# A two-layer trunk of three token mixers: state-space and output splits in slots of their own, the norm gain spread by products, a longer pause of the table work

## The chip, the core and the metric

The kernel runs on one core of a Trainium2 chip. The metric is the device time of one execution in microseconds (us), the median of several runs.

## What is computed

A residual stream x of 512 tokens by 1024 channels passes two layers. Cut to what matters here, a layer is:

```
h = rmsnorm(x, norm_g)                      # norm_g: 1024 gains, one row a layer
proj = h @ w_in                             # split into rq rk rv rz, sq sk sv sz, cu cz, ga gb gc
y_a = retention(rq, rk, rv) * silu(rz)      # 4 heads, chunks of 128
y_b = stick_breaking(sq, sk, sv) * silu(sz) # 8 heads of 64, strictly causal
y_c = s5_ssm(cu) * silu(cz)                 # scan over a complex state, gelu, then
                                            # y * sigmoid(y @ w_glu + b_glu)
merged = sigmoid(ga) * (y_a @ proj_a) + sigmoid(gb) * (y_b @ proj_b) + sigmoid(gc) * (y_c @ proj_c)
x = x + merged @ w_out
```

All is float32. A float32 product of large operands is made of three products of a 32-bit format that TensorE takes in one pass: each operand is split into a high part (a ScalarE copy, names ending in h) and a low part (operand minus high part, on VectorE, names ending in l), and hh, hl and lh are summed.

## The kernel before

**Slots.** A layer is a list of 108 main pieces, written out in `ORDER_TEXT`; a piece is 12 or 24 products of 512 columns (`mm`) that fill one PSUM bank. Here a slot is one piece with all that is emitted around it. The loop at the end of `layer` (from L1342) writes a slot in this order: first the helpers that are due (generators in `due`), then the piece, then the helpers' second halves (those that yielded 0, in `late`), then `W.fill()`, which splits coming weights (`wh` on ScalarE, `wl` on VectorE; weights are loaded as `raw` on SP's queue), then background work. A helper that yields n goes on n slots later. Nothing reorders after that: each engine runs its instructions in the order in which they were written, and waits on semaphores.

**Background.** In layer 0 it is `tables()` (powers of the state matrix, small VectorE products with buffers `dbl`, tables `cr`, `ci`, `fr`, `fi`) and then `coef.gen` (L672 on: coefficients of the scan, GpSimd products `ct`, `bbr`, `bbi`, `ab`, from four loads of 256 KB that ScalarE's queue issues); in layer 1 it is `coef.gen` alone. The loop pulls steps while two counters of emitted work, of GpSimd and of VectorE, stay below shares of the slot's TensorE work; a step that has nothing to do yet only raises the counter. In the slots of `quiet` (L1341) nothing is pulled: the slot of the first attention pair and the one before, and six slots at the fourth pair.

**Attention pairs.** `sb_pair(pr)` (L1017), pr 0 to 3, starts every four slots from the last `sv` on. It copies `qd` and `ks` on ScalarE and `ql`, `ks` on VectorE, and a GpSimd copy completes each `qd`. Then, slot by slot and for two heads, TensorE makes scores (`z`), ScalarE two sigmoids (`kp`, `w`), VectorE a scan over `kp` and the product into `w`, and TensorE turns `w` by transposes (`wt`), so TensorE waits for VectorE's `w` there. At its end the pair's output `sbo` is multiplied by the gate and split at once into `ybh`, `ybl`; they are read by the `pb` pieces, the first of them 13 slots after the first pair's split and five after that of the third.

**State space.** `ssm(q)` (L872), q 0 to 3, makes the branch's output `g[q]`. When q is 3, its end splits all four `g` into `gh`, `gl` in one slot (L955 on), waits two slots (`K["s7"]`) and multiplies each `g` by its gate `zc` on GpSimd. The `glu` pieces, after the four slots of `rv1`, read the splits; `glu_evac` multiplies `g` again. The split stands in the slot of the last `rv0`, where `W.fill` also makes the four weight units of `rv1`.

**Start.** `first_x` (L430) normalises the four token blocks of x. The gain must lie on all 128 partitions (`gB`, two tiles of 512 columns); `load_gain` (L424) reads the one row of 2 KB 128 times, by a broadcasting transfer for each tile, behind the first block of x in SP's queue and ahead of the first weights. A block is squared on ScalarE, its mean and root on GpSimd (`rs`), scaled on VectorE (`xn`), transposed on TensorE (`T`) and copied as `hh` and `hl`.

Of the kernel before, what the change touches and what calls it, by code (L numbers as in the profile page):

```python
# [10 lines left out]
F32 = mybir.dt.float32  # L11
# [3 lines left out]
ALU = mybir.AluOpType  # L15
PSUM = bass.MemoryType.PSUM

P = 128
# [17 lines left out]
K = dict(  # L36

    nw=12, w=4, raw=4, b=48,

    sb0=0, sb_gap=4, ssm0=6, ssm_gap=3, ret0=9, ret_gap=3, x0=-3, x1=2, ret_pre=4, lead=15,  # L40

    g=0.9, v=0.7,

    n1=1, n2=1, q1=1, q2=1, k1=1, k2=2, s1=1, s2=1, s3=1, s4=2, s5=1, s6=1, s7=2, b1=1, b2=1, b3=1,
# [142 lines left out]
def trunk(ctx: ExitStack, tc, x_in, w_in, par_in, bc_in, ng_in, cst_in, rope_in, out):  # L187
    nc = tc.nc
    load = {"V": 0.0, "G": 0.0, "T": 0.0}

    def counted(f, engine, each):


        def g(*a, **k):
            o = k["out"] if "out" in k else a[0]
            load[engine] += 0.07 * (engine != "T") + each * math.prod(o.shape[1:])
            return f(*a, **k)  # L197

        return g
# [4 lines left out]
    GT, GS = counted(nc.gpsimd.tensor_tensor, "G", 2.2e-3), counted(nc.gpsimd.tensor_scalar, "G", 1.2e-3)  # L204
# [11 lines left out]
    def bt(name, dt=F32, shape=(P, 512)):  # L216
        return bp.tile(list(shape), dt, tag="b", name=name)
# [7 lines left out]
    def psm(name):  # L225
        return ps_sm.tile([P, 512], F32, tag="sm", name=name)
# [14 lines left out]
    def C(n):  # L241
        o, s = CST[n]
        return cst[:, o : o + s]

    make_identity(nc, ident)
    make_identity(nc, identb)
    nc.gpsimd.memset(negm, -1e30)
    nc.gpsimd.affine_select(
        out=negm, in_=negm, pattern=[[1, P]], base=0, channel_multiplier=-1, compare_op=ALU.is_ge, fill=0.0
# [31 lines left out]
    def split(src, name, shape=(P, 512)):  # L281
        h = bt(name + "h", F32R, shape)
        l = bt(name + "l", F32R, shape)
        ACT(h, src, AF.Copy)  # L284
        TT(out=l, in0=src, in1=h.bitcast(F32), op=ALU.subtract)
        return h, l
# [137 lines left out]
    def load_gain(l, q=nc.scalar):  # L424
        gB = [bt("gB0"), bt("gB1")]
        for c in range(2):
            q.dma_start(out=gB[c], in_=ng_in[l, 512 * c : 512 * c + 512].partition_broadcast(P))
        return gB

    def first_x():  # L430
        xs = [[bt("x0"), bt("x1")] for t in range(NT)]
        gB = []

        def load(t):
            for c in range(2):
                nc.sync.dma_start(out=xs[t][c], in_=x_in[t * P : t * P + P, 512 * c : 512 * c + 512])

        load(0)
        gB.extend(load_gain(0, nc.sync))
        W.load(2)  # L440
        load(1)
        W.load(4)

        def block(t):
            ss = st("ss", 2)
            xn = [sum_square(xs[t][c], ss, c) for c in range(2)]
            yield from normalise(t, xs[t], xn, ss, gB)

        b = [block(t) for t in range(NT)]
        for i in range(3):  # L450
            next(b[0])
        W.make()
        next(b[0], None)
        next(b[1])
        W.make()
        next(b[1])
        load(2)
        W.make()
        load(3)
        W.make()  # L460

        def second():
            next(b[1])
            next(b[1], None)

        between.append(second)
        next(b[2])
        spawn(b[2], 0)
        spawn(b[3], 0)
# [340 lines left out]
    def layer(l, last, base):  # L810
# [59 lines left out]
        g = [None] * 4  # L870

        def ssm(q):  # L872
            win, ca, mt, T = coef.q[q]
            p0 = G * l + 8 * q

            pu = transposed(U[q])
            yield 0
            ut = bt("ut")
            for k in range(2):
                src = pu[64 * k : 64 * k + 64].rearrange("p (i c j) -> p i c j", i=4, j=2)  # L880
                for j in range(2):
                    dst = ut[64 * j : 64 * j + 64].rearrange("p (i k c) -> p i k c", i=4, k=2)
                    ACT(dst[:, :, k, :], src[:, :, :, j], AF.Copy)
            yield K["s1"]
            ps = psm("S")
            for n in range(8):
                sl = slice(n * 64, n * 64 + 64)
                MM(ps[:, sl], win[n // 4][:, n % 4 * P : n % 4 * P + P], ut[:, sl], start=True, stop=True)
            yield 0

            H, tm, tx = bt("H"), bt("tm"), bt("tx")
            lo, hi = slice(0, 64), slice(64, P)
            TT(out=tm, in0=ps, in1=T[0], op=ALU.mult)
            TT(out=tx[lo], in0=ps[hi], in1=T[1][hi], op=ALU.mult)
            TT(out=tx[hi], in0=ps[lo], in1=T[1][lo], op=ALU.mult)
            yield K["s2"]
            TT(out=tm, in0=tm, in1=tx, op=ALU.add)
            for n in range(8):
                sl = slice(n * 64, n * 64 + 64)
                nc.vector.tensor_tensor_scan(  # L900
                    tm[:, sl], r8[:, p0 + n : p0 + n + 1].to_broadcast([P, 64]), tm[:, sl], 0.0, ALU.mult, ALU.add
                )
            nc.gpsimd.memset(v3(H, 64)[:, :, 0:1], 0.0)
            yield K["s3"]

            def sh0(ap):
                return v3(ap, 64)[:, :, 0:63]

            def sh1(ap):
                return v3(ap, 64)[:, :, 1:64]  # L910


            TT(out=sh1(H), in0=sh0(tm), in1=sh0(T[0]), op=ALU.mult)
            TT(out=sh0(tx)[lo], in0=sh0(tm)[hi], in1=sh0(T[1])[hi], op=ALU.mult)
            TT(out=sh0(tx)[hi], in0=sh0(tm)[lo], in1=sh0(T[1])[lo], op=ALU.mult)
            TT(out=sh1(H), in0=sh1(H), in1=sh0(tx), op=ALU.subtract)
            yield K["s4"]

            py = psm("py")
            for i in range(4):  # L920

                for part in range(2):
                    for n in (i, i + 4):
                        sl = slice(n * 64, n * 64 + 64)
                        o = py[64 * (n // 4) : 64 * (n // 4) + 64, n % 4 * P : n % 4 * P + P]
                        k = 2 * (n % 2) + n // 4
                        if part == 0:
                            MM(o, ut[:, sl], mt[n % 4 // 2][:, k * P : k * P + P], start=True, stop=False)
                        else:
                            MM(o, H[:, sl], ca[:, n, 1:9, :].rearrange("p a b -> p (a b)"), start=False, stop=True)  # L930
            coef.used = q + 1
            yield 0
            ysb = bt("ysb")
            ACT(
                ysb.rearrange("p (j g m) -> p g j m", j=8, g=4), py.rearrange("p (g j m) -> p g j m", g=4, j=8), AF.Copy
            )
            yield K["s5"]
            pt = transposed(ysb)
            yield 0
            y = bt("y")  # L940
            for k in range(2):
                src = pt[64 * k : 64 * k + 64].rearrange("p (i h c) -> p i h c", i=4, h=2)
                for h in range(2):
                    dst = y[64 * h : 64 * h + 64].rearrange("p (c i k) -> p i c k", i=4, k=2)
                    ACT(dst[:, :, :, k], src[:, :, h, :], AF.Copy)

            u, sg = bt("gu"), bt("gs")
            ACT(u, y, AF.Square, scale=math.sqrt(0.044715))
            yield K["s6"]
            STT(out=u, in0=u, scalar=1.0, in1=y, op0=ALU.add, op1=ALU.mult)  # L950
            yield 0
            ACT(sg, u, AF.Sigmoid, scale=2.0 * math.sqrt(2.0 / math.pi))
            TT(out=y, in0=y, in1=sg, op=ALU.mult)
            g[q] = y
            if q == 3:  # L955
                yield 1
                for i in range(4):
                    gs[i] = split(g[i], "g")
                yield K["s7"]
                for i in range(4):  # L960
                    while zc[i] is None:
                        yield 1
                    GT(out=g[i], in0=g[i], in1=zc[i], op=ALU.mult)


        gs, yc, yb, mg, ya = [None] * 4, [None] * 4, [None] * 4, [None] * 8, [None] * 8
        zc, zb = [None] * 4, [None] * 4
# [49 lines left out]
        def sb_pair(pr):  # L1017
# [85 lines left out]
            for kb in range(4):  # L1103

                for h in range(2):
                    c = slice(128 * pr + 64 * h, 128 * pr + 64 * h + 64)
# [6 lines left out]
            while zb[pr] is None:  # L1113
                yield 1
            TT(out=sbo[pr], in0=sbo[pr], in1=zb[pr], op=ALU.mult)
            yb[pr] = split(sbo[pr], "yb")


# [127 lines left out]
        gB = []  # L1246
# [91 lines left out]

        first = at["sv"] + 3 + K["sb0"]
        turn = first + 3 * K["sb_gap"]  # L1340
        quiet = {*range(first - 1, first + 1), *range(turn, turn + 6)}  # L1341
        for name, m in mains:  # L1342
            i = now[0]
            quarters()
# [21 lines left out]
    while due:  # L1366
        i = min(due)
# [28 lines left out]
```

## Time and profile before

| | |
|---|---|
| median of three runs | 1303.77 us (1303.42 to 1303.91) |
| the profiled execution | 1303.42 us, its span 1301.7 us |
| TensorE (PE) busy | 1267.4 us, 97% of the span |
| VectorE (DVE) busy | 853.3 us, 66% |
| ScalarE (ACT) busy | 537.5 us, 41% |
| GpSimd (POOL) busy | 391.3 us, 30% |
| moved by DMA | 120.05 MB, mean 92 GB/s |

The page comes from one execution. PE is TensorE's products, PEld its weight loads. An engine's idle time matters only where it makes TensorE wait. Views with times are given from the span's start. The two layers run the same list of pieces, so layer 1 (from 661 us on) can be laid beside layer 0 (from 11 us on); a slot's length below is the time from its first product with weights to that of the next slot.

### The profile page before, as it was taken

What the parts mean: (1) busy time and instruction counts of PE and PEld (TensorE: products, weight loads), DVE (VectorE), ACT (ScalarE), POOL (GpSimd) and SP (SyncE); (2) the same over time, 40 slices, a digit from 0 to 9 for tenths busy, and PEclk for the clock granted to TensorE, in tenths of its full rate; (3) what the DMA queues carried; (4) which work ended last, traced back from release to release, by engine and by line L of the source; (5) the groups of instructions that cost most, each with busy time, mean ns of one, the idle gap of its engine ahead of it and who ended that gap; (6) DMA issues with size and microseconds to landing.
All of it is one profiled execution on the core that took longest, in us unless ns stands there. A gap on an engine that the chain in (4) does not pass through costs nothing. (4 is left out here: it accounts for less than half of the span.)

```text
span 1301.7 us, 16635 instructions
## 1 busy us (share of the span) xinstructions
PE 1267.4 (97%) x6360; PEld 1048.0 (81%) x6360; DVE 853.3 (66%) x1189; ACT 537.5 (41%) x919; POOL 391.3 (30%) x452
## 2 busy tenths in 40 slices
PE   7997999999999999999999998999999999999998
PEld 5886778888887888888888876888888878888887
DVE  5988795866785539556365578678657844575542
ACT  5453455445343533332244544534534534423311
POOL 3334351638442012000043136444565311210000
PEclk9998999999999999999999999999999999999999
DMA  6331222223322322234433222122232232122342
GB/s 225 94 134 49 65 68 75 69 82 97 114 65 65 113 78 69 81 97 142 162 118 129 81 66 65 49 82 81 89 106 65 74 121 82 65 81 81 97 135 75
DMA packets 37375, 120.05 MB, mean 92 GB/s; under 512 B 4144, under 2 KB 4528, under 8 KB 37296
## 3 DMA queue, kind: packets, MB, share of 16 engines
q1 hardware_dynamic: 29664, 105.40, 25.6%
q10 hardware_dynamic: 7632, 13.59, 3.1%
q8 instruction: 50, 0.82, 0.3%
q14 instruction: 29, 0.24, 0.1%
HBM read 114.78 MB, written 4.19 MB: 91 GB/s over the span
## 5 line engine op out<-in xcount | busy, mean ns | idle before, releaser
L197 DVE TENSOR_TENSOR wl<-raw,wh 128x1024 fp32r<-128x1024 f32 x196 | 253.6, 1302 | 115.8 <-ACT wh L318 112.8
L197 PE MATMUL mm<-hh,wh 128*128 128x512 f32 x640 | 256.4, 401 | 0.0
L197 PE MATMUL mm<-hh,wl 128*128 128x512 f32 x640 | 251.1, 392 | 0.0
L197 PE MATMUL mm<-hl,wh 128*128 128x512 f32 x640 | 251.0, 392 | 0.0
L318 ACT ACTIVATE wh<-raw 128x1024 fp32r<-128x1024 f32 x196 | 205.8, 1057 | 71.4 <-PE mm L197 38.9
L197 PE MATMUL mm<-wh,hh 128*128 128x512 f32 x512 | 206.6, 404 | 0.6 <-ACT hh L421 0.6
L197 PE MATMUL mm<-wl,hh 128*128 128x512 f32 x512 | 201.9, 394 | 4.3 <-DVE wl L197 4.3
L197 PE MATMUL mm<-wh,hl 128*128 128x512 f32 x512 | 201.4, 393 | 0.0
L197 PEld LDWEIGHTS mm<-hh,wh 128*128 128x128 f32 x640 | 121.1, 189 | 25.6 <-issue 1.8
L197 PEld LDWEIGHTS mm<-hh,wl 128*128 128x128 f32 x640 | 120.8, 189 | 26.0
L197 PEld LDWEIGHTS mm<-hl,wh 128*128 128x128 f32 x640 | 121.1, 189 | 23.4
L197 PEld LDWEIGHTS mm<-wl,hh 128*128 128x128 f32 x512 | 104.6, 204 | 24.3 <-DVE wl L197 7.9
L197 PEld LDWEIGHTS mm<-wh,hh 128*128 128x128 f32 x512 | 104.5, 204 | 18.0 <-ACT hh L421 1.0
L197 PEld LDWEIGHTS mm<-wh,hl 128*128 128x128 f32 x512 | 104.3, 204 | 18.0 <-DVE hl L197 0.3
L994 ACT ACTIVATE gate<-mm 128x512 f32<-128x512 f32 x48 | 28.6, 596 | 117.2 <-PE mm L197 117.2
L1051 DVE TENSOR_TENSOR_SCAN kp<-kp,zero 128x511 f32<-128x511 f32 (+1 forms) x64 | 59.8, 955 | 21.3 <-ACT kp L1047 21.2
L197 POOL TENSOR_SCALAR ms<-ss 128x8 f32<-128x8 f32 (+3 forms) x56 | 19.1, 341 | 181.7 <-DVE ss L824 100.9
L197 POOL TENSOR_TENSOR rs<-ms,mhalf 128x8 f32<-128x8 f32 (+3 forms) x56 | 64.7, 1155 | 4.7
L822 ACT ACTIVATE sq<-mm 128x512 f32<-128x512 f32 x32 | 19.0, 592 | 84.6 <-PE mm L197 84.5
L197 PE MATMUL mm<-wl,mgh 128*128 128x512 f32 x128 | 50.1, 391 | 0.2
L197 PE MATMUL mm<-wh,mgh 128*128 128x512 f32 x128 | 49.9, 390 | 0.0
L197 PE MATMUL mm<-wh,mgl 128*128 128x512 f32 x128 | 49.9, 390 | 0.0
(253 smaller groups left out, 2240.1 us busy)
## 6 DMA issues: line engine op xcount, KB each, us to landing
raw<-in_w SPq DMA_DIRECT2D x196, 512.0 KB, 3.5
x<-in_x SPq DMA_DIRECT2D x8, 256.0 KB, 7.3
rope<-in_rope ACTq DMA_DIRECT2D x8, 256.0 KB, 3.9
xh<-in_x ACTq DMA_DIRECT2D x8, 256.0 KB, 4.3
x<-xh ACTq DMA_DIRECT2D x8, 256.0 KB, 2.2
xh<-x ACTq DMA_DIRECT2D x8, 256.0 KB, 4.1
out<-xh ACTq DMA_DIRECT2D x8, 256.0 KB, 2.0
gB<-in_ng SPq DMA_DIRECT2D x2, 256.0 KB, 6.3
```

Of the source, the lines that this page charges most:

```text
L197: return f(*a, **k)
L318: ACT(wh, raw, AF.Copy)
L822: ACT(s2, ps, AF.Square)
L994: ACT(sg, ps, AF.Sigmoid)
L1051: nc.vector.tensor_tensor_scan(v, v, zero1.to_broadcast([P, n - 1]), 1.0, ALU.mult, ALU.add)
```

## The change

Four edits:

- The gain of layer 0 is loaded as two rows of 2 KB on one partition by ScalarE's queue, and two products of a column of ones with them spread it over the partitions; VectorE copies it to `gB`. The broadcasting transfers go from SP's queue. (Layer 1's gain is loaded as before.)
- At the end of `ssm(3)` each of the four splits has a slot of its own, and the product of a `g` with its gate follows a slot behind its split.
- In `sb_pair` 0, 1 and 2 the split of the output goes to the slot after the product with the gate.
- `quiet` at the first pair is two slots longer.

```diff
+    ones = bt("ones", F32, (1, P))
+    nc.gpsimd.memset(ones, 1.0)
...
+        rows = [bt("grow", F32, (1, 512)) for c in range(2)]
+
+        def spread_gain():
+            for c in range(2):
+                pg = psm("gain")
+                nc.tensor.matmul(pg, ones, rows[c], start=True, stop=True)
+                gB.append(bt(f"gB{c}"))
+                nc.vector.tensor_copy(out=gB[c], in_=pg)
...
+        for c in range(2):
+            nc.scalar.dma_start(out=rows[c], in_=ng_in[0:1, 512 * c : 512 * c + 512])
         load(0)
-        gB.extend(load_gain(0, nc.sync))
+        spread_gain()
         W.load(2)
...
             if q == 3:
+                for i in range(4):
+                    yield 1
+                    gs[i] = split(g[i], "g")
+                    if i:
+                        while zc[i - 1] is None:
+                            yield 1
+                        GT(out=g[i - 1], in0=g[i - 1], in1=zc[i - 1], op=ALU.mult)
                 yield 1
-                for i in range(4):
-                    gs[i] = split(g[i], "g")
-                yield K["s7"]
-                for i in range(4):
-                    while zc[i] is None:
-                        yield 1
-                    GT(out=g[i], in0=g[i], in1=zc[i], op=ALU.mult)
+                GT(out=g[3], in0=g[3], in1=zc[3], op=ALU.mult)
...
             TT(out=sbo[pr], in0=sbo[pr], in1=zb[pr], op=ALU.mult)
+            if pr < 3:
+                yield 1
             yb[pr] = split(sbo[pr], "yb")
...
-        quiet = {*range(first - 1, first + 1), *range(turn, turn + 6)}
+        quiet = {*range(first - 1, first + 3), *range(turn, turn + 6)}
```

How it moves instructions is read from the built programs. VectorE in layer 0, the slots of `sz:1` and `sz:0`, before: behind the first pair's scan and weights (`kp`, `w`) stand twelve table products, six of 128x128 and six of 128x192, of which the first eight are shown.

```order
L1051 SCALAR_TENSOR_TENSOR kp<-kp,zero_85 128x511
L197 TENSOR_TENSOR w_1018<-w_1018,kp 128x511
L197 TENSOR_TENSOR dbl_605<-cr 128x128
L197 TENSOR_TENSOR dbl_606<-ci 128x128
L197 TENSOR_TENSOR dbl_607<-cr,ci 128x128
L197 TENSOR_TENSOR cr<-dbl_605,dbl_606 128x64x2
L197 TENSOR_TENSOR dbl_605<-ci,cr 128x128
L197 TENSOR_TENSOR ci<-dbl_607,dbl_605 128x64x2
L197 TENSOR_TENSOR dbl_605<-cr 128x192
L197 TENSOR_TENSOR dbl_606<-ci 128x192
```

VectorE in layer 0 now, the slot of `gb:0`: the table products begin behind the weights' `wl` of that slot.

```order
L1065 SCALAR_TENSOR_TENSOR kp<-kp,zero_85 128x511
L197 TENSOR_TENSOR w_1136<-w_1136,kp 128x511
L1089 COPY wt_1143<-wt 128x512
L197 TENSOR_TENSOR wl<-raw,wh 128x1024
L197 TENSOR_TENSOR dbl_615<-cr 128x128
L197 TENSOR_TENSOR dbl_616<-ci 128x128
L197 TENSOR_TENSOR dbl_617<-cr,ci 128x128
L197 TENSOR_TENSOR cr<-dbl_615,dbl_616 128x64x2
```

They moved past 12 instructions: past the rest of the first pair's weights and two `wl`. On GpSimd the eight coefficient operations move behind the second pair's two `qd` copies; in layer 1 neither engine's order changes at these slots.

VectorE at the end of `ssm(3)`, layer 0, before (the same in layer 1): `gl` is the low part of a state-space split, `m` belongs to `rk`.

```order
L197 TENSOR_TENSOR y<-y,gs 128x512
L197 TENSOR_TENSOR m_3632<-m_3632,m_3633 128x512
L197 TENSOR_TENSOR gl<-y,gh 128x512 x4
L197 TENSOR_TENSOR wl<-raw,wh 128x1024 x4
L197 TENSOR_TENSOR m_3676<-m_3676,m_3677 128x512
L197 TENSOR_TENSOR m_3728<-m_3728,m_3729 128x512
```

VectorE at the same place now.

```order
L197 TENSOR_TENSOR y<-y,gs 128x512
L197 TENSOR_TENSOR m_3642<-m_3642,m_3643 128x512
L197 TENSOR_TENSOR gl<-y,gh 128x512
L197 TENSOR_TENSOR wl<-raw,wh 128x1024 x4
L197 TENSOR_TENSOR m_3686<-m_3686,m_3687 128x512
L197 TENSOR_TENSOR gl<-y,gh 128x512
L197 TENSOR_TENSOR m_3738<-m_3738,m_3739 128x512
L197 TENSOR_TENSOR gl<-y,gh 128x512 x2
L197 TENSOR_TENSOR wl<-raw,wh 128x1024 x4
```

Three of the four `gl` moved from ahead of the four `wl` to behind them, each into a later slot.

ScalarE at the slot of `gb:5`, layer 0, before (the same in layer 1): `gate` empties a finished piece, `ybh` is the high part of the second pair's output, `win` copies transposed coefficients out of PSUM.

```order
L994 ACTIVATE gate<-mm 128x512
L284 ACTIVATE ybh<-sbo 128x512
L729 ACTIVATE win_1745<-T_1688 128x512
L729 ACTIVATE win_1747<-T_1693 128x512
L1047 ACTIVATE kp<-z_1698 128x512
L1048 ACTIVATE w_1749<-z_1698 128x512
```

ScalarE now, the slots of `gb:5` and `gb:6`.

```order
L1008 ACTIVATE gate<-mm 128x512
L742 ACTIVATE win_1751<-T_1698 128x512
L742 ACTIVATE win_1753<-T_1703 128x512
L1061 ACTIVATE kp<-z_1708 128x512
L1062 ACTIVATE w_1755<-z_1708 128x512
```

```order
L1008 ACTIVATE gate<-mm 128x512
L1042 ACTIVATE qd_1789<-sqk 64x512
L1043 ACTIVATE ks_1791<-sqk 64x512
L1042 ACTIVATE qd_1790<-sqk 64x512
L1043 ACTIVATE ks_1792<-sqk 64x512
L286 ACTIVATE ybh<-sbo 128x512
L1061 ACTIVATE kp<-z_1811 128x512
L1062 ACTIVATE w_1856<-z_1811 128x512
```

`ybh` moved from ahead of `win` to the next slot, behind the fourth pair's `qd` and `ks` and ahead of the third pair's sigmoids; `ybl` stands on VectorE in the same way, behind the `ql` and `ks` and ahead of the scans.

## Rows read from the trace of the kernel before

**Rows 1.** The page, part 1: busy us (share) and instructions of each engine.
```profile
PE 1267.4 (97%) x6360; PEld 1048.0 (81%) x6360; DVE 853.3 (66%) x1189; ACT 537.5 (41%) x919; POOL 391.3 (30%) x452
```

**Rows 2.** Waits of PE: line waited for: us in total, times, longest.
```profile
PE wt L1068 <- DVE w L197: 12.3, 8, 6.0
PE T L398 <- DVE xn L197: 8.9, 1, 8.9
PE mm L197 <- DVE wl L197: 4.3, 4, 1.6
PE wt L1068 <- ACT win L729: 4.1, 2, 2.1
```

**Rows 3.** Windows, `sz:0` and `gb:0`, layers 0, 1: us, busy PE PEld DVE ACT POOL, clock.
```profile
93.43:116.33 22.90, 16.25 (x73) 13.12 (x72) 18.23 (x25) 6.84 (x13) 8.32 (x9) 0.85 0.17 63
739.45:753.17 13.72, 13.72 (x72) 11.31 (x72) 8.86 (x12) 6.61 (x13) 0.00 (x0) 1.00 0.27 78
```

**Rows 4.** Timeline of DVE, layer 0: start, us, operation, [idle before <-releaser].
```profile
94.12 1.15 DVE L197 TENSOR_TENSOR dbl<-cr 128x128 f32<-128x128 f32 x1
...
101.66 0.35 DVE L197 TENSOR_TENSOR dbl<-cr,ci 128x192 f32<-128x192 f32 x1
...
102.97 0.69 DVE L197 TENSOR_TENSOR silu<-mm,silu 128x512 f32<-128x512 f32 x1
```

**Rows 5.** Timeline of DVE, layer 1: the second pair's `ql`.
```profile
753.46 0.68 DVE L197 TENSOR_TENSOR ql<-sqk,qd 64x512 fp32r<-64x512 f32 x1 [3.27 <-ACT qd L1028]
```

**Rows 6.** Timeline of POOL, layer 1: the second pair's first `qd` copy.
```profile
753.49 1.12 POOL L1033 CAST qd<-qd 64x512 fp32r<-64x512 f32 x1 [21.77 <-ACT qd L1028]
```

**Rows 7.** Windows: the first and the second slot of `rv1`, layer 0.
```profile
404.02:412.68 8.66, 6.51 (x31) 4.81 (x30) 7.79 (x6) 2.79 (x5) 3.14 (x2) 1.00 0.48 141
412.68:418.61 5.93, 5.93 (x31) 4.90 (x30) 0.00 (x0) 1.09 (x3) 0.00 (x0) 1.00 0.15 60
```

**Rows 8.** Timeline of DVE, layer 0, before and in the first slot of `rv1`.
```profile
399.08 4.71 DVE L197 TENSOR_TENSOR gl<-y,gh 128x512 fp32r<-128x512 f32 x4 [3.76 <-ACT gh L284]
403.71 6.98 DVE L197 TENSOR_TENSOR wl<-raw,wh 128x1024 fp32r<-128x1024 f32 x4
```

**Rows 9.** Timeline of ACT, layer 1, the slot of `gb:5`.
```profile
811.54 0.63 ACT L284 ACTIVATE ybh<-sbo 128x512 fp32r<-128x512 f32 x1 [2.54 <-DVE sbo L197]
812.07 1.07 ACT L729 ACTIVATE win<-T 128x512 f32<-128x512 f32 x2
```

**Rows 10.** Windows: from `gb:5`'s first product to `gb:6`'s, layers 1, 0.
```profile
812.90:821.82 8.92, 8.92 (x51) 7.01 (x51) 6.66 (x6) 4.41 (x9) 6.10 (x6) 0.81 0.15 38
176.29:183.61 7.32, 7.32 (x52) 5.88 (x51) 6.67 (x6) 4.42 (x9) 6.11 (x6) 1.00 0.00 1
```

**Rows 11.** Timeline of DVE, layer 1, slots of `gb:3`, `gb:1` and `gb:5`.
```profile
777.73 0.69 DVE L197 TENSOR_TENSOR ybl<-sbo,ybh 128x512 fp32r<-128x512 f32 x1 [3.31 <-ACT ybh L284]
...
784.82 0.68 DVE L197 TENSOR_TENSOR ql<-sqk,qd 64x512 fp32r<-64x512 f32 x1 [2.13 <-ACT qd L1028]
...
812.20 1.49 DVE L197 TENSOR_TENSOR ybl<-sbo,ybh 128x512 fp32r<-128x512 f32 x1 [0.69 <-ACT ybh L284]
```

**Rows 12.** Timeline of DVE, the start.
```profile
8.06 1.42 DVE L197 SCALAR_TENSOR_TENSOR xn<-x,rs,gB 128x512 f32<-128x512 f32 x2 [8.06 <-DMA gB<-in_ng]
```

**Rows 13.** Timeline of PE, the start: the first product with weights.
```profile
11.44 0.80 PE L197 MATMUL mm<-wh,hh 128*128 128x512 f32 x1 [0.60 <-ACT hh L421]
```

**Rows 14.** Timeline of ACT, the start.
```profile
3.41 0.63 ACT L404 ACTIVATE xn<-x 128x512 f32<-128x512 f32 x1 [1.32 <-DMA x<-in_x]
...
9.84 1.06 ACT L318 ACTIVATE wh<-raw 128x1024 fp32r<-128x1024 f32 x1 [5.07 <-DMA raw<-in_w]
```

**Rows 15.** Timeline of SP's queue, the start: the first two issues.
```profile
0.81 0.86 SPq L436 DMA_DIRECT2D x<-in_x  x2
```

**Rows 16.** PE's groups by form: xcount | busy us, mean ns | idle before.
```profile
L197 PE MATMUL mm<-wh,hh 128*128 128x512 f32 x512 | 206.6, 404 | 0.6 <-ACT hh L421 0.6
...
L197 PE MATMUL sbo<-wt,sv 128*64 128x512 f32 x32 | 8.6, 618 | 0.0
```

## The prediction, made before the changed kernel ran

> **What bounds the kernel now.** I read the page's busy times first, then what TensorE waited for, then stretches of slots side by side. TensorE is busy 97% of the span [rows 1], so a term counts only where it removes a wait of TensorE, or some of its work, or adds one. Its waits are few and large [rows 2]: 12.3 us for `w` from VectorE (eight waits, the longest 6.0), 8.9 us at the start for the first normalised block, 4.3 us for `wl` (four waits), 4.1 us for `win` from ScalarE (two waits). The second view compares the layers: both run the same slots, so a slot that is longer in layer 0 shows what only layer 0 carries there. The change touches a place of each of these four kinds.
>
> **Tables, two slots later (layer 0).** The slots of `sz:0` and `gb:0` take 22.90 us in layer 0 and 13.72 in layer 1 [rows 3]. The difference, 9.18 us, is the tail of the tables: twelve VectorE products stand ahead of the attention weights that TensorE turns next. They run from 94.12 to 102.97, 8.85 us, mostly at over 1 us each, because GpSimd's coefficient products run beside them; the last four of them, 128x192, take 1.31 us from 101.66 to 102.97 when GpSimd has gone on to other work [rows 4], or 0.33 each. The new order puts the twelve behind the `wl` of `gb:0` and ahead of the second pair's `ql`. Layer 1 shows that place: VectorE is idle for 3.27 us there, until ScalarE's `qd` [rows 5], and GpSimd for 21.77 [rows 6]; in layer 0 GpSimd will be idle there too, since its coefficient products now stand behind that pair's copies. Twelve at 0.33 are 3.9 us, and six of them are a third smaller, so they about fill that idle time. I take **-9.2 us**; bounds -8.5 (0.6 over 3.27, all of it paid, and a little for the loads) and -9.9 (the products that ran beside the second pair's weights are gone from that slot, and as much is won there). In layer 1 the longer pause moves nothing: there the order of VectorE and GpSimd around these slots is as before.
>
> What queues behind: GpSimd gets eleven products and two scalings between the second and third pair's `qd` copies, where it had five. It stands idle long enough to take them, and the copies have a slot until the scores need them. On ScalarE the four loads of coefficients are issued behind the `wh` of `gb:2`, where ScalarE otherwise waits for TensorE: nothing.
>
> **State-space splits, a slot each (both layers).** The first slot of `rv1` lasts 8.66 us, the next, with the same work, 5.93 [rows 7]. In it TensorE waits for `wl`: VectorE does four `gl` in 4.71 us and only then four `wl` in 6.98 [rows 8], both stretched by GpSimd's products beside them (3.14 us busy in that window, [rows 7]). Now one `gl` and at most one product stand ahead of the four `wl`, and three `gl` move to slots where VectorE is idle (0.00 busy in the second window of [rows 7]). Three `gl` less are 3.5 us at their stretched price and 2.1 at the 0.69 of such a split alone [rows 11], against a wait of 2.73, and `wl` shrinks too. The fourth `wh` waits for a `wl` itself, so a rest may stay. **-2 x 2.73 = -5.5 us**; bounds -4.0 and -5.6. The last `gl` and its product are done a slot before `glu` reads them.
>
> **Output splits, a slot later (pairs 0 to 2, both layers).** What is won: in the slot of `gb:5`, ScalarE's queue holds `ybh`, then the two copies `win`. `ybh` waits 2.54 us for VectorE's `sbo`, and `win` stands behind it [rows 9]; TensorE needs the bank that `win` frees, and waits (4.1 us in two layers, [rows 2]). With `ybh` gone, `win` follows the gate's copy and lands before TensorE asks. **-4.1 us.** In layer 1 that wait is followed by a stretch at half clock: the slot behind it takes 8.92 us with a granted clock of 0.81, against 7.32 at 1.00 in layer 0 [rows 10]. Without the wait I expect full clock: **-1.6 us**.
>
> What is paid: `ybl` (0.69 us, [rows 11]) now stands ahead of the next slot's scans, and from a pair's `ql` on VectorE runs without a pause to the `w` for which TensorE waits. Ahead of the third pair's `ql` it is idle for 2.13 us [rows 11], but `ybl` stands behind that `ql`, so the idle time covers nothing. I charge 0.6 in the slots of `gb:1` and `gb:6`, and 0.3 in that of the last `cu`, where TensorE comes to `w` a little after it is there: 1.5 a layer, **+3.0 us**; bounds 0 and +4.1 (six times 0.69). A 0.63 us `ybh` is also put before a scan's input, but VectorE is the later of the two.
>
> **Start.** The first normalisation begins at 8.06 with the wait for `gB` [rows 12]. But the first product, at 11.44 [rows 13], stands behind `hh`, which ScalarE does after `wh`, and `wh` began at 9.84 with the landing of the first weights [rows 14]. So an earlier gain alone would win little; what counts is that two transfers of 256 KB each go from the head of SP's queue, and the weights move up by two places. ScalarE now issues two rows of 2 KB ahead of its table load. The first `x`, 256 KB, was issued at 0.81 [rows 15] and worked on at 3.41 [rows 14]; I take 3.2 for both rows to be there. The spreading costs two f32 products of 512 columns, each of which the trace has as two instructions of 618 ns at full clock [rows 16]; that is 1.2 us, and 2.5 at half clock, with overlap. At the start TensorE is at half clock (its first 512-column instruction takes 0.80, [rows 13], against a mean of 0.40, [rows 16]), so 1.7 each. With the copy to `gB` (0.9, estimate from a PSUM operation of this size) xn begins at 3.2 + 3.4 + 0.9 = 7.5, half a microsecond earlier; from xn to the first product are 0.8 to the transposes, 0.9 for four of them, 0.6 for `hh`, some 2.4: 9.9 to 10.0. **-1.4 us**; bounds +0.2 (2.5 each) and -2.0 (1.2 each).
>
> **The sum**, against the profiled execution's 1303.42 (span 1301.7 and 1.7 around it): -9.2 - 5.5 - 4.1 - 1.6 + 3.0 - 1.4 = -18.8, or 1284.6. The median of the runs shown lies 0.35 above that execution, so I forecast **1285.0**.
>
> **A rule weighed.** `ybl` takes 0.69 us with GpSimd quiet and 1.49 beside its products [rows 11]: 0.8 more. Layer 0 now has eleven such products in the slots of `gb:2` to `gb:3`, where it had five a slot earlier. If five more VectorE instructions meet one, that is 4.0 us, of which the idle 2.13 us before the third pair's `ql` [rows 11] hide half: +1.9. The Trainium skill, "SBUF — State Buffer", section "Who interferes with whom", says that a VectorE instruction with two SBUF inputs and a GpSimd instruction that reads SBUF lock each other out for a whole instruction. By that rule the work moved to GpSimd would hold up VectorE wherever it lands, which speaks against this part; the trace agrees where both run. I take 0, since these slots' VectorE work is light, and keep +1.9 as a rival.
>
> **Rivals.** (1) The sum holds: 1285.0, chance 0.54; alone it spans 1281 to 1288. (2) The clock falls in one or two of the waits that remain (for the weights in the slots of `gb:1` and `gb:6`, which grow by 0.6): 1.6 each [rows 10]. For it: the same 2 us wait did so in layer 1. Against: it did not in layer 0. 1286.6 to 1288.2, chance 0.19. (3) GpSimd holds up VectorE in layer 0, +1.9: 1286.9, chance 0.11. (4) The start stays, because the rows land late or the products are slow: 1286.4, chance 0.08. (5) `win` is late for another reason, its transposes or a bank: 4.1 and 1.6 stay, 1290.7, chance 0.05. Against: the trace has `win` 0.5 us behind the start of `ybh`. (6) The other side: VectorE's backlog is conserved. If VectorE has no idle time behind the new places, each moved piece is paid at the next wait of TensorE, and `ybl` adds 3.0: 1303.8 + 3.0 = 1306.8, slower. It decides where the moved work exceeds the idle time behind it: for the tables 3.9 against 3.27, but 8.85 if GpSimd runs beside them [rows 4], and that comes true only if its products start before the second pair's copies, which stand ahead of them in its queue. Chance 0.02. A rest of 0.01 is for no change.
>
> **The numbers.** The range runs from the best of (1), `ybl` costing nothing (-3.0), the start at -2.0 (-0.6) and the tables at -9.9 (-0.7), 1280.7, to (5): **1280.5 to 1291.0**. 0.2% of the time, 2.6 us, is about what a measurement of this kernel can tell from no change; all cases but (6) and the rest are faster by more: 0.97, 0.01, 0.02.
>
> **What would show it.** Right: the two slots of [rows 3] near 13.7 us in layer 0; the longest wait for `w` down from 6.0 to under 2; no wait for `win` and a clock of 1.00 in the slot of `gb:5`; the first slot of `rv1` near 6.0; `w` waits behind `gb:1` and `gb:6` about 0.6 longer; the first product near 10.0 with `wh` no longer the last to come. Wrong: `ql` of the second pair in layer 0 over 1 us behind `qd`, third-pair scores waiting for `qd`, a new half-clock stretch, or the first product still behind the weights.

## The result and the profile after

The changed kernel takes 1292.09 us (median of four, 1288.97 to 1292.46), the kernel before beside it 1303.84: a ratio of 0.9905, 95% interval 0.9894 to 0.9917. It is faster, as forecast, but by 11.7 us in place of 18.8, and 1292.09 lies above the forecast's upper end of 1291.0. The profiled execution took 1292.46 with a span of 1290.7, 11.0 under the span of before.

What TensorE waited for, after (line, releaser: us in total, times, longest):

```profile
PE wt L1082 <- DVE w L197: 10.2, 9, 2.1
PE gain L441 <- DMA grow<-in_ng: 2.5, 1, 2.5
PE T L400 <- DVE xn L197: 1.4, 1, 1.4
PE mm L197 <- DVE wl L197: 0.5, 1, 0.5
```

Against [rows 2], the waits for `win` and nearly all of those for `wl` are gone, and the start waits 3.9 in place of 8.9. The wait for `w` is the surprise: its longest piece fell from 6.0 to 2.1 as forecast, yet the total fell by 2.1 only, and there are nine. So new waits have come. Where they are, windows of single slots show (us, busy PE PEld DVE ACT POOL with counts, clock, DMA share, GB/s); after, in order: `sz:0` and `gb:0` of layer 0; `gb:1`, `gb:4` of layer 0; the first slot of `rv1`; then of layer 1 `sz:2`, `gb:2`, `gb:1`, `gb:4`, `gb:7`, `gb:5`, `gb:6`. (The wait for `win` ends the stretch of `gb:7`: the helpers of the slot of `gb:5` are written ahead of its first product.)

```profile
92.92:106.65 13.73, 13.73 (x74) 11.32 (x72) 11.88 (x24) 6.63 (x13) 0.00 (x0) 1.00 0.26 78
137.83:148.11 10.28, 8.04 (x39) 6.49 (x39) 9.60 (x12) 7.26 (x14) 6.28 (x9) 0.95 0.31 102
148.11:158.27 10.16, 10.16 (x52) 7.39 (x50) 10.06 (x8) 4.49 (x8) 9.16 (x6) 0.88 0.17 52
395.07:401.00 5.93, 5.93 (x32) 4.90 (x30) 3.88 (x5) 2.50 (x5) 1.67 (x1) 1.00 0.80 254
741.51:753.35 11.84, 8.39 (x40) 6.85 (x39) 11.22 (x12) 6.83 (x13) 10.26 (x8) 0.91 0.15 45
753.35:762.97 9.62, 9.62 (x52) 7.04 (x50) 5.44 (x7) 4.44 (x8) 0.69 (x2) 0.93 0.18 55
776.73:787.30 10.57, 8.40 (x40) 6.86 (x39) 9.94 (x12) 7.30 (x14) 5.96 (x7) 0.91 0.15 51
787.30:797.00 9.70, 9.70 (x51) 7.06 (x49) 9.60 (x8) 4.49 (x8) 9.42 (x6) 0.92 0.18 56
797.00:805.06 8.06, 8.06 (x48) 6.72 (x46) 7.44 (x12) 2.26 (x6) 3.06 (x5) 1.00 0.16 45
805.06:812.38 7.32, 7.32 (x53) 5.88 (x51) 5.30 (x5) 3.52 (x7) 6.81 (x6) 1.00 0.19 55
812.38:820.50 8.12, 7.33 (x42) 5.92 (x38) 7.71 (x13) 6.74 (x13) 1.90 (x3) 1.00 0.25 91
```

The same view of before, for the slots that [rows 3], [rows 7] and [rows 10] don't hold: `gb:1` and `gb:4` of layer 0; `sz:2`, `gb:2`, `gb:1`, `gb:4`, `gb:7` and `gb:6` of layer 1.

```profile
147.69:156.88 9.19, 7.51 (x39) 5.97 (x39) 8.50 (x10) 6.66 (x13) 5.04 (x7) 1.00 0.29 103
156.88:165.93 9.05, 9.05 (x52) 6.56 (x50) 8.95 (x8) 4.72 (x9) 8.89 (x6) 1.00 0.19 58
...
753.17:761.73 8.56, 7.34 (x41) 5.91 (x39) 7.97 (x10) 6.62 (x13) 4.99 (x5) 1.00 0.21 63
761.73:770.76 9.03, 9.03 (x52) 6.55 (x50) 7.42 (x9) 4.65 (x9) 7.13 (x5) 1.00 0.20 58
784.53:793.53 9.00, 7.51 (x40) 5.97 (x39) 8.38 (x10) 6.67 (x13) 5.74 (x7) 1.00 0.30 104
793.53:802.58 9.05, 9.05 (x52) 6.56 (x50) 8.95 (x8) 4.65 (x9) 8.89 (x6) 1.00 0.19 60
802.58:812.90 10.32, 8.28 (x48) 6.71 (x46) 9.38 (x13) 2.04 (x5) 4.49 (x6) 1.00 0.17 51
821.82:829.15 7.33, 7.33 (x41) 5.92 (x38) 6.92 (x12) 5.55 (x11) 2.43 (x3) 1.00 0.16 42
```

The gains stand where they were forecast: 22.90 to 13.73 [rows 3], 8.66 to 5.93 [rows 7], 10.32 to 8.06 in `gb:7`, 8.92 to 7.32 [rows 10]. The losses are in three pairs of neighbouring slots: 3.3 and 0.6 us in `sz:2` and `gb:2` of layer 1, 1.1 and 1.1 in `gb:1` and `gb:4` of layer 0, 1.6 and 0.65 in the same slots of layer 1; in each pair the clock column falls below 1.00, a stretch at 1.2 GHz in place of 2.4. In the first pair TensorE did this before the fall:

```profile
749.87 0.30 PE L1082 MATMUL wt<-ident,w 128*128 128x128 f32 x1 [2.11 <-DVE w L197]
751.51 2.18 PE L1082 MATMUL wt<-ident,w 128*128 128x128 f32 x9 [1.34 <-DVE w L197]
```

Two waits for `w`, 3.5 us with one transpose between them; before, the waits of this slot came to 1.2 (8.56 less the 7.34 that PE is busy). In that slot GpSimd is busy for 10.26 us where it had 4.99. Its rows, after (start, us, operation, [idle before <-releaser]):

```profile
743.59 1.10 POOL L1047 CAST qd<-qd 64x512 fp32r<-64x512 f32 x1
744.77 1.40 POOL L197 TENSOR_TENSOR ab<-bbr,y_re 128x512 f32<-128x512 f32 x1
746.13 1.18 POOL L197 TENSOR_TENSOR ct<-bbi,y_im 128x512 f32<-128x512 f32 x1
747.38 1.79 POOL L197 TENSOR_TENSOR ab<-ab,ct 128x512 f32<-128x512 f32 x1
```

And VectorE's, where `w` is what TensorE waits for:

```profile
745.27 2.85 DVE L1065 TENSOR_TENSOR_SCAN kp<-kp,zero 128x127 f32<-128x127 f32 x2
748.22 1.50 DVE L197 TENSOR_TENSOR w<-w,kp 128x511 f32<-128x511 f32 x1
```

The coefficient product `ab` follows the `qd` copies without a pause. GpSimd's order of instructions there is that of before. But GpSimd's waits of before in that slot (line, releaser: us, times, longest) hold this:

```profile
POOL ab L197 <- DVE w L197: 2.8, 1, 2.8
```

The product reads nothing of `w`. It waited for its buffer. Most tiles share one pool of 48 buffers (the ring, below), and a tile gets a buffer that an earlier tile has done with: in the program of before this product may begin when VectorE's `w` has read the `kp` that held the buffer. After the change it gets the buffer of another tenant, a `sqk`, which VectorE's `ql` has read four instructions ahead of that `w`.

### The profile page after: what moved, and what is told of

Read it like the earlier page. It is cut to its first block, busy times and chain, and to the rows that moved or that the text cites. A ratio compares the mean times of both kernels' runs of the same rounds, so it can differ in the third digit from the quotient of the medians.

```text
span 1290.7 us, 16658 instructions
## 1 busy us (share of the span) xinstructions
PE 1271.7 (99%) x6364; PEld 1051.5 (81%) x6364; DVE 844.7 (65%) x1191; ACT 537.1 (42%) x919; POOL 390.1 (30%) x453
## 4 chain that ended last, share of the span: by engine, by line
PE 82%; DVE 3%; ACT 1%; issue 0%; DVEq 0%; ACTq 0%
PE mm L197 71%; PE T L400 2%; PE ro L197 2%; PE py L197 1%; PE wt L1082 1%; DVE kp L1065 1%; PE S L197 1%; PE sbo L197 1%; PE z L197 1%; DVE w L197 1%; PE rkv L197 1%; PE rs L197 1%; PE yaT L1251 1%; DVE ks L197 0%; DVE ybl L197 0%
## 5 line engine op out<-in xcount | busy, mean ns | idle before, releaser
L197 DVE TENSOR_TENSOR wl<-raw,wh 128x1024 fp32r<-128x1024 f32 x196 | 249.3, 1279 | 101.8 <-ACT wh L320 98.2
```

## The experiments

Theory: the deferred output splits take their two buffers later, so the later tiles of the ring shift; GpSimd's first product in layer 1 starts inside VectorE's scans and slows them (3.9 us); the waits of `gb:1`, longer by `ybl`, bring half-clock slots in both layers (3 us); and the start's clock was slow to rise in the profiled execution. Rivals: the order of VectorE's work itself; the splits as such; the start.

**e1, buffers alone.** Two unused buffers are taken where the first pair's split took its two.

```diff
             if pr < 3:
+                for i in range(2 if pr == 0 else 0):
+                    nc.gpsimd.memset(bt("pad")[:, 0:1], 0.0)
                 yield 1
```

> The changed kernel, with two unused buffers taken (a one-column memset on GpSimd each) at the place where the first pair's output split used to take its two. Every instruction of the change stays in its place; only the later buffers of the ring shift by two, so that in layer 1 the first coefficient product of GpSimd again gets a buffer that VectorE's last `w` of that slot has to release. Theory (the coefficient product runs beside VectorE's scans because its buffer is free earlier): the slot of sz:2 in layer 1 goes back from 11.84 to about 8.6 us and the next from 9.62 to about 9.0, some 3.9 us in all: 1288.2. Rival A (the slot is long because the deferred ybl or the new order of VectorE's work delays the weights): the slot stays near 11.8 us and the time at 1292. Rival B (the clock alone fell there by chance): the product stays early and the slot changes without it.

Measured: 1287.01 us (1285.58 to 1287.66; the kernel before beside it 1303.56; ratio 0.9867, 0.9851 to 0.9883). Windows of `sz:2` and `gb:2`, layer 1:

```profile
739.46:748.04 8.58, 7.34 (x41) 5.91 (x39) 7.96 (x10) 6.62 (x13) 5.06 (x7) 1.00 0.19 62
748.04:757.08 9.04, 9.04 (x53) 6.56 (x51) 7.43 (x9) 4.66 (x9) 7.13 (x5) 1.00 0.19 59
```

GpSimd and VectorE of that slot:

```profile
745.44 1.30 POOL L197 TENSOR_TENSOR ab<-bbr,y_re 128x512 f32<-128x512 f32 x1 [2.72 <-DVE w L197]
```

```profile
743.23 1.27 DVE L1065 TENSOR_TENSOR_SCAN kp<-kp,zero 128x127 f32<-128x127 f32 x2
744.60 0.69 DVE L197 TENSOR_TENSOR w<-w,kp 128x511 f32<-128x511 f32 x1
```

With the deferred `ybl` still in its place, the product waits again (2.72 us; the two memsets ahead of it take 0.13), the scans take 1.27 in place of 2.85, `w` 0.69 in place of 1.50, and the two slots are those of before: 3.84 us. That settles the buffer against rivals A and B; e2, without memsets, has these slots back too. The rest of the 5.9 us between the two profiled spans is not this: here `gb:1` and `gb:4` of layer 0 take 9.77 and 9.05 at full clock (1.6 less), the first slot 10.37 (1.3 less), and `gb:6` of layer 0 is 0.8 longer.

**e2, the second pair alone.**

```diff
-            if pr < 3:
+            if pr == 1:
                 yield 1
```

> The changed kernel with only the second pair's output split deferred (the one behind which ScalarE's win stood); the first and third pair's are done where the kernel before does them. Theory (what is lost in the slots of gb:1, gb:4, sz:2 and the last cu comes from the first and the third pair's deferred split, the win gain from the second alone): gb:1 -1.1 and -1.6 us, the half-clock slot behind each -1.1 and -0.65, sz:2 and gb:2 of layer 1 -3.9 (their buffers are back as well), the last cu -0.35 twice; gb:7 stays at 8 us. Sum -9.0: 1283.1, faster than both kernels. Rival (only the buffers matter; gb:1 is longer for another reason): 1288. Rival (the win wait comes back, because it takes the first pair's deferral too): gb:7 at 10.3 us in both layers, 1288 to 1290.

Measured: 1284.59 us (1283.66 to 1285.04; ratio 0.9847, 0.9829 to 0.9865). Windows: `gb:1` and `gb:4` of layer 0, then `sz:2` and `gb:7` of layer 1:

```profile
136.49:146.77 10.28, 7.87 (x40) 6.33 (x39) 9.95 (x13) 6.86 (x13) 6.07 (x7) 0.96 0.32 102
146.77:157.07 10.30, 10.30 (x52) 7.47 (x50) 10.20 (x8) 4.50 (x8) 9.32 (x6) 0.87 0.17 51
...
740.09:748.66 8.57, 7.34 (x41) 5.91 (x39) 7.98 (x10) 6.62 (x13) 5.00 (x5) 1.00 0.21 64
789.51:797.57 8.06, 8.06 (x48) 6.72 (x46) 7.82 (x11) 2.32 (x6) 3.42 (x5) 1.00 0.00 0
```

In layer 1 `sz:2` (8.57) and `gb:1` (9.00) are those of before, as the theory said, and the `win` wait stays away, so the second pair's deferral alone carries its gain. In layer 0 the theory missed: `gb:1` and `gb:4` stay long without the first pair's `ybl`, so something else lengthens that wait (e3, e6). Some 7.5 of the 9.0 us were won.

**e3, no deferral.** The two lines `if pr < 3: yield 1` are taken out.

> The changed kernel with all output splits back at their old place; tables, state-space splits and start stay. Theory: the wait for win returns (gb:7 +2.3 twice, and a half-clock slot behind it in layer 1, +1.6), and what the deferral cost goes (sz:2 and gb:2 of layer 1 -3.9, gb:1 -2.7, half-clock slots -1.8, gb:6 -1.6, last cu -0.7): 1287.7, so that deferring all three splits loses 4.4 us. Rival (the forecast's own sum, deferral gains 2.7): 1294.8.

Measured: 1285.89 us (1285.58 to 1287.29; ratio 0.9862, 0.9846 to 0.9878). `gb:1` of layer 0 and `gb:5` of layer 1:

```profile
136.70:146.25 9.55, 7.52 (x40) 5.97 (x39) 9.22 (x11) 6.64 (x13) 5.65 (x8) 1.00 0.35 110
...
799.46:808.37 8.91, 8.91 (x51) 7.02 (x50) 6.66 (x6) 4.41 (x9) 6.09 (x6) 0.81 0.16 41
```

The `win` wait (`gb:7` of layer 1 at 10.31) and its half-clock slot are back, and still this kernel is some 6 us faster than the changed one. Deferring all three splits, which the forecast had at -2.7 us, cost about that much by the medians, more than the theory's 4.4; of the 5.1 us between the two profiled spans the slots that the deferral touches hold 4.0 and the start, where the clock rose at 11.3 here, 1.1. In layer 0 `gb:1` is 9.55, 0.35 over before, without any deferral and here at full clock.

**e4, the old start.** The `ones`, `rows` and `spread_gain` lines go, and:

```diff
-        spread_gain()
+        gB.extend(load_gain(0, nc.sync))
```

> The changed kernel with the start of the kernel before: the gain comes broadcast by two transfers on SP's queue, no spreading products. Theory (the new start brings the first product 2.0 us forward, and TensorE gives 1.5 of it back in the first slot, at half clock until 17.4 us and waiting for the second unit's wl): 0.5 us slower, 1292.6; first product at 11.4, first slot 10.1 us, the clock rises at 15.4. Rival (the forecast's term, 1.4): 1293.5. Rival (the new start only adds half-clock time): 1291 or less. The slots of layer 1 stay as in the changed kernel if the three buffers that the start takes have no part in sz:2; if they have, sz:2 goes to 8.6 and the time to 1288.7.

Measured: 1293.12 us (1291.84 to 1294.38; ratio 0.9915, 0.9898 to 0.9932), 1.0 over the changed kernel and 1.2 over its second measurement (e5), too near for this run to size. The first slot takes 10.87 us from 11.71, and full clock came only at 18.4. `sz:2` stays at 11.84, so the start's three buffers have no part in it. In `gb:1` of layer 1 the clock happened to hold:

```profile
779.65:789.36 9.71, 7.52 (x40) 5.98 (x39) 9.09 (x11) 7.08 (x14) 5.56 (x7) 1.00 0.19 54
789.36:798.41 9.05, 9.05 (x53) 6.55 (x50) 8.95 (x8) 4.71 (x9) 8.89 (x6) 1.00 0.19 60
```

That separates the two causes in that slot: `ybl` is worth 0.71 (9.71 against 9.00), its own 0.69 us, and the half clock the other 1.5 (20.27 against 18.76 for the two slots).

**e5, the changed kernel again.** No edit.

> The changed kernel itself, once more, for its start and its clock. Theory (the new start is worth the forecast's 1.4 us or more, and the profiled execution of the result had TensorE's full clock late, at 17.4 us, where three kernels with the same start have had it at 11.2, 11.3 and 12.9): the first slot takes 10.4 to 10.7 us in place of 11.64, and the time of the profiled execution is lower by as much as the half-clock stretches are fewer; the slots of sz:2 (11.8) and gb:1 (10.5) in layer 1 stay long. Rival (the late clock belongs to this program): 11.6 us again, clock up at 17.4.

Measured: 1291.89 us (1291.45 to 1293.27; ratio 0.9911, 0.9894 to 0.9927). The first slot takes 10.45 us in place of 11.64, with full clock from 13.2 in place of 17.4; `sz:2` (11.74) and `gb:1` (10.44) of layer 1 are long again, and the same three pairs of slots have their half clock. The late rise belonged to that execution. The three stretches came again in this one, but one run of the changed kernel, at 1288.97 us, speaks against their coming every time (below).

**e6, the pause alone, on the kernel before.**

```diff
-        quiet = {*range(first - 1, first + 1), *range(turn, turn + 6)}
+        quiet = {*range(first - 1, first + 3), *range(turn, turn + 6)}
```

> The kernel before with the longer pause of the tables alone. Theory: sz:0 and gb:0 of layer 0 at 7.1 and 6.6 us (-9.2); the slot of gb:1 in layer 0 0.35 to 1.1 us longer, because GpSimd's coefficient products now stand ahead of the third pair's copies, with or without a half-clock slot behind it (+1.2); layer 1 as in the kernel before, sz:2 at 8.55. 1303.5 - 9.2 + 0.4 to 2.3 = 1294.7 to 1296.6. Rival (the longer gb:1 of layer 0 comes from the other parts): 1294.3, gb:1 at 9.2.

Measured: 1293.69 us (1293.23 to 1294.04; before 1303.50; ratio 0.9921, 0.9906 to 0.9936). `sz:0` with `gb:0`, then `gb:1`, layer 0, and `sz:2` of layer 1:

```profile
93.06:106.78 13.72, 13.72 (x72) 11.30 (x72) 11.87 (x24) 6.61 (x13) 0.00 (x0) 1.00 0.23 77
...
137.93:147.48 9.55, 7.51 (x39) 5.97 (x39) 9.21 (x11) 6.64 (x13) 5.64 (x8) 1.00 0.34 110
...
743.71:752.26 8.55, 7.33 (x40) 5.90 (x39) 7.96 (x10) 6.61 (x13) 4.98 (x5) 1.00 0.17 63
```

-9.2 in the two slots (the time is 1.0 under the theory's lower end); `sz:2` of layer 1 is that of before, so the pause has no part in its 3.3 us. And +0.35 in `gb:1` of layer 0, as in e3: the price of the pause there. VectorE shows it, before and here:

```profile
148.04 1.11 DVE L197 TENSOR_TENSOR ql<-sqk,qd 64x512 fp32r<-64x512 f32 x1 [2.21 <-ACT qd L1028]
...
137.25 1.48 DVE L197 TENSOR_TENSOR wl<-raw,wh 128x1024 fp32r<-128x1024 f32 x1
138.66 1.09 DVE L197 TENSOR_TENSOR ql<-sqk,qd 64x512 fp32r<-64x512 f32 x1
```

The third pair's `ql` begins 0.73 us into the slot where it began at 0.35. GpSimd's delayed coefficient products now run beside the VectorE work ahead of it (that `wl` took 1.22 before), and the idle 2.21 us are used up.

**e7, the state-space splits undone.** The block `if q == 3` of the diff above is put back.

> The changed kernel with the state-space splits as in the kernel before (four in a row, then the four products). Theory: only the first slots of rv1 change, 5.93 to 8.66 us in each layer: +5.4, 1297.5. Rival (part of the wait came from the other edits): a first slot of rv1 below 8 us.

Measured: 1296.55 us (1295.66 to 1297.18; ratio 0.9943, 0.9928 to 0.9957), 4.7 over e5, which ran beside it. The first slots of `rv1` take 8.6 in both layers again, +2.7 each; one of them:

```profile
393.81:402.44 8.63, 6.51 (x32) 4.82 (x30) 7.78 (x6) 2.81 (x5) 3.13 (x2) 1.00 0.48 141
```

**e8, the second pair's split behind `win`, in its own slot.**

```diff
-            if pr < 3:
-                yield 1
+            if pr == 1:
+                yield 0
+                yield 0
```

> As e2, but the second pair's output split is not put a slot later: it is done at the end of its own slot, on ScalarE behind both win, the two sigmoids and the copies of turned weights, on VectorE behind the copy of turned weights and ahead of the next wl. Theory (what the second pair's split costs in the slot of gb:6 is its place ahead of that slot's scans; ahead of the pair's ql VectorE has idle time that covers it): gb:7 stays at 8.05, gb:6 goes from 8.13 and 8.58 to 7.33 in both layers, -2.0: 1282.5. Rival (VectorE's backlog is conserved, ybl is paid wherever it stands before the scans): gb:6 stays near 8.1, 1284.6. Rival (ScalarE's later ybh holds up the fourth pair's qd): gb:5 or gb:6 longer than 8.1, slower than 1284.6.

Measured: 1283.80 us (1283.15 to 1284.16; ratio 0.9845, 0.983 to 0.9859). `gb:6` of layers 0 and 1:

```profile
172.37:179.90 7.53, 7.33 (x41) 5.92 (x38) 7.12 (x12) 5.75 (x11) 1.91 (x3) 1.00 0.30 92
...
804.14:812.51 8.37, 7.54 (x42) 6.00 (x38) 7.96 (x12) 6.60 (x13) 3.40 (x5) 1.00 0.38 123
```

In layer 0 0.6 of the 0.8 in `gb:6` is gone, where the theory had all of it; in layer 1 only 0.2 of 1.25 (e2 had 8.13 and 8.58 there). There GpSimd is late: its product `ab` runs into the fourth pair's `ql` on VectorE. Here, and before:

```profile
802.79 2.05 POOL L197 TENSOR_TENSOR ab<-bbr,y_re 128x512 f32<-128x512 f32 x1
803.84 1.55 DVE L197 TENSOR_TENSOR ql<-sqk,qd 64x512 fp32r<-64x512 f32 x1
...
821.47 0.68 DVE L197 TENSOR_TENSOR ql<-sqk,qd 64x512 fp32r<-64x512 f32 x1 [2.15 <-ACT qd L1028]
```

`ql` takes 1.55 us in place of 0.68, and the scans start 4.2 us into the slot in place of 3.1. The two slots ahead are 3.9 us shorter than before (2.3 and 1.6), while GpSimd has as much to do from `gb:7` to `gb:6` (12.9 us busy against 13.0): part of what the `win` wait gave back was paid here. This is read from the trace; no run tested it.

**e9 to e11: the start on top of e8.** e9 is e8 with the edit of e4; e11 is e8 once more; e10 adds one product to e8:

```diff
         spread_gain()
+        nc.tensor.matmul(psm("warm")[:, 0:256], ones, rows[1][:, 0:256], start=True, stop=True)
```

> The kernel of e8 with the start of the kernel before (gain broadcast by two transfers on SP's queue). Layers as in e8. Theory (the new start is worth about the forecast's 1.4 us once the luck of the clock is averaged out: second slot at 19.8 to 20.0 in four of five executions with it, 21.6 and 22.6 without): 1.0 to 2.0 us slower than e8, some 1285.3, the second slot starting at 21 to 22.6. Rival (TensorE gives the earlier first product back at half clock, as in the profiled execution of the result): within 0.5 us of e8.

> The kernel of e8 with one more spreading product of 256 columns into a bank that nobody reads, behind the two of the gain, in TensorE's gap between 6.2 and 7.5 us. Theory (full clock at the start comes earlier if TensorE does not pause before the first transposes): clock up by 11.2 us in the profiled execution, first slot 10.4 or less, 0 to 1 us faster than e8. Rival (when the clock rises does not hang on that gap): first slot between 10.4 and 11.6 as before, no difference; the products delay the transposes by under 0.3.

> The kernel of e8 once more, on the same chip as e9 and e10, to compare with them: 1283 to 1284.

Measured side by side (the kernel before 1305.78): e9 1286.07 (1284.88 to 1286.20; ratio 0.9851, 0.9838 to 0.9864), e10 1283.56 (1283.07 to 1284.78; 0.9837, 0.9823 to 0.985), e11 1284.01 (1283.62 to 1284.19; 0.9838, 0.9825 to 0.9852). The new start is worth 2.1 us by the medians of e9 and e11, at the theory's upper end; e9's rival falls. The second slot starts at 22.32 in e9 and 20.13 in e11. Over all profiled executions it starts at 20.1 on average in the eight with the new start alone, and at 21.9 in the four with the old one. e10 shows no difference that these runs can tell, and its clock rose at 16.4, so that theory falls.

The best kernels are e2, e8 and e10, at 1283.6 to 1284.6; between them the intervals decide nothing, and all are some 8 us faster than the changed kernel.

## Why the forecast was right in direction and wrong in size

By slots of the two profiled executions, against the kernel before:

| step of the prediction | forecast | measured |
|---|---|---|
| tables | -9.2 | -9.2 (and -0.2 in `sz:2`, +0.35 in `gb:1`, e6) |
| state-space splits | -5.5 | -5.4 |
| `win` wait, and the clock behind it | -4.1, -1.6 | -4.6, -1.6 |
| `ybl` ahead of scans | +3.0 | +3.2 (0.7 and 0.2 in `gb:1`, 0.8 twice in `gb:6`, 0.36 twice in the last `cu`) |
| start | -1.4 | -0.5 here; -2.1 by e9 and e11 |
| layer 1, `sz:2` and `gb:2` | 0 | +3.9 |
| half clock behind `gb:1`, both layers | 0 | +3.1 (1.6 by e1 in layer 0, 1.5 by e4 in layer 1) |
| sum | -18.8 | -11.0 |

**The step that failed** is the price of the deferred output splits, "What is paid": +3.0 with a bound of +4.1, which made the whole deferral a gain of 2.7. It counts nothing but the `ybl` on VectorE. That the first pair's split takes its two buffers a slot later, and that other work then starts sooner, stands at nothing in the sum, without a reason. With that, GpSimd's coefficient product in `sz:2` of layer 1 lost its wait for a buffer, ran into VectorE's scans, and 3.9 us went in `sz:2` and `gb:2`; e1 gives back 3.84 of them by two unused buffers, with all else of the change in place. With this and the half-clock stretch behind `gb:1` of layer 1 the deferral's parts come to a loss of 2.4 us in place of the gain of 2.7, and to 4.0 with the stretch of layer 0, which came without it too. The prediction's one sentence on these slots, "In layer 1 the longer pause moves nothing: there the order of VectorE and GpSimd around these slots is as before", holds for the pause (e6: `sz:2` at 8.55) and for the order; what it did not ask is whether the start of GpSimd's product is held by the order or by a buffer.

Rival (3) had the mechanism, GpSimd beside VectorE, but in layer 0 and at 1.9 us; there it was 0.35 (e6), which the prediction put at nothing because "these slots' VectorE work is light". The rule weighed, the Trainium skill, "SBUF — State Buffer", section "Who interferes with whom", told what it would do once it happened, and the trace agrees: beside products of 1.18 to 1.79 us, two scans that take 1.27 us together took 2.85, and a `w` of 0.69 took 1.50.

**Rival (2)**, given 0.19, came true in both layers, at `gb:1` and not at `gb:6`, at its price of 1.6 each. The weight against it was that a 2 us wait, the one for `win`, had kept full clock in layer 0. At that place it did so again wherever the wait was left (e3, e6), and layer 1 fell each time; at `gb:1` of layer 0 it falls out either way. Of the 12 profiled executions with the longer pause, 9 had half clock behind the wait of `gb:1` in layer 0; e3 had not and e8 had, with the same instructions in the same order up to there. So layer 0 needs no deferral for it: the longer pause alone had brought that wait from 1.7 us to 2.0 (e6), and five of the seven executions with the first pair's split at its old place fell. In layer 1, where the deferral alone makes the wait longer (1.5 to 2.2 us), four of the five with it fell and none of the eight without. Over runs it shows too: the one run of the changed kernel at 1288.97 us has a mean clock of 0.999, the others 0.996.

**The start** was sized somewhat small: 2.1 us by e9 and e11, 1.8 by the starts of the second slot in 12 executions, 1.0 to 1.2 by e4, against 1.4. The rows were there sooner than assumed (the first spreading product began at 2.46, not 3.2) and the copy to `gB` took 0.69, not the 0.9 for which the prediction shows no row: `xn` began at 6.86 in place of the forecast 7.5. (Two products at 1.2 in place of 1.7 would have put the bound at -2.4, not -2.0.) The profiled execution hid the gain. Its first product came 1.98 us sooner (11.44 to 9.46), but TensorE stayed at half clock until 17.4 us, as its products show:

```profile
15.61 0.63 PE L197 MATMUL mm<-wh,hl 128*128 128x512 f32 x1
...
17.79 0.39 PE L197 MATMUL mm<-wl,hh 128*128 128x512 f32 x1
```

and its first slot took 11.64 us where seven other executions with that start took 10.4 to 10.7. That most of the start's gain is missing from the profiled execution is bad luck, not a fault of the term.

**Right** were the tables, the state-space splits, the `win` wait with its clock, and the 0.7 us or so for each `ybl` that stands ahead of scans (0.2 in `gb:1` of layer 0). One reading behind the tables was loose: of the twelve products before, four took over 1 us (1.15 to 1.41), not most; the term came out all the same, since the twelve took 3.7 us in their new place. That the deferral as a whole loses (2.4 to 4.0 us by slots, about 6 by the medians of e3) the prediction did not see; it summed it to a gain of 2.7.

## What to carry to other kernels

Where tiles share one pool of buffers, moving a tile's first write by a slot re-deals the later buffers: for off-path work that an engine does "when it has time", look up what it waited for before, and if it was a buffer, count that wait as protection that the change may remove. A wait of TensorE that grows to about 2 us should be priced with the half-clock stretch behind it (1.5 to 1.6 us here) at better than even odds, and a place that keeps full clock in one execution can lose it in the next, as `gb:1` of layer 0 did. To keep a gain, defer only the piece that stands in the way: the second pair's split alone kept all of the `win` gain, and `sz:2` and `gb:2` of layer 1 stayed those of before (e2).

## What was not expected of the hardware

When TensorE's clock reaches its full level at the start varies by some 6 us between executions of one start: 11.2, 11.3, 12.5, 12.8, 12.9, 13.2, 15.5 and 17.4 us in the eight with the new start alone. With the old one, which begins its products 2 us later, it was 15.4, 16.0, 17.7 and 18.4, and 16.4 where one more product filled TensorE's gap ahead of the first transposes. (Before the first rise the clock column of a window shows 1.00, so the length of the products tells.) The first slot took 10.4 to 10.7 us with the new start as long as the rise came by 15.5 us, and 11.64 with 17.4, so a start is compared over several executions. And VectorE's scans are held up beside GpSimd's products as its own products are (2.85 us against 1.27, e1), though a scan's second input is one column that is broadcast.
